# Rows of 320 columns for the feed-forward's split input, and a ten-column tile of ones

## The chip, the cores and the metric

The kernel runs on one core of one Trainium2 chip. The metric is the time of one execution on the device, in microseconds (us). Three executions of the kernel before took 365.12, 365.38 and 365.51 us; the median is 365.38 us.

## The reference

One transformer block on 256 tokens of width 1024, in float32. What matters here is its last part:

```
x = x + gate1 * (merged @ w_out)
h = rmsnorm(x, g_ffn) * (1 + scale2) + shift2
x = x + gate2 * (square(relu(h @ w_ff1)) @ w_ff2)
return rmsnorm(x, g_final)
```

`w_ff1` is 1024 x 4096 and `w_ff2` 4096 x 1024. Ahead of this stand the modulation (six vectors of 1024 out of `c @ w_ada`), the input projection, attention, a spatial gating unit and the two gates `ga` and `gb`, which weigh the outputs of the two branches into `merged`.

## The kernel before

Activations lie transposed: 128 features on the partitions, `KT` = 8 blocks of features, 256 tokens along a row. Each float32 product is made of three products in the format `float32r`: a weight tile `raw` is split into a high part `whi` (a rounded copy, by ACT) and a low part `wlo` (the rest, by DVE), an activation in the same way, and `mm3` issues high x high, low activation x high weight, high activation x low weight into one PSUM bank. The activation is the moving operand, the weights are loaded into the array for each matmul, 128 columns at a time.

The feed-forward's input is `zh` (high) and `zl` (low), one row of each for each block `ko` of features. A row holds 256 tokens and two columns more, `ZW` = 258: column 256 carries the shift of the modulation, so that its product with the weights comes out of the same matmul, and column 257 is zero. (The norm's factor of each token is applied behind the product, in `relu2`.) `zh` and `zl` use the room of `ga_sb` and `gb_sb`, the two gates, by the same tags `b3` and `b4`, and those in turn the room of the tiles `xn` and `xt` of the start.

`ff1(n)` makes 256 of the 4096 hidden features: for each `ko` in order and each half `i` one `mm3`, so six matmuls on row `ko`, 48 in a call, into two banks. `relu2` and `relu2_low` turn the result into `fh` and `fl`, 512 columns of which a matmul reads 256. `ff2(n)` adds their product with 256 rows of `w_ff2` into four banks, again 48 matmuls a call. There are 16 calls of each; past the start they alternate, `ff2(n)` then `ff1(n + 3)`. Instructions of each engine stand in the order in which the text issues them where `InOrder` is pinned, and PE's follows the calls above. `prepare` loads and splits weight tiles two slots ahead, all loads on SP's queue.

The tile `ones` is read in two places: `ones[:, 0:1]` is the moving operand that sums squares over features (`sums`), and `ones[:, 0:2]` is an operand of a first GpSimd operation at the start (L140). Attention and the projections (`wide`, with rows of `hh`, `hl`, `oh`, `yh`, `mh` and others, 256 columns each) run ahead of the feed-forward.

Tiles get their room in the order of the pools: first `const`, in which `ones` lies, then `act` with `b3` and `b4`, then the pools of work tiles and of weights. Each tile begins at a multiple of 32 bytes. What follows a tile moves when its size changes.

Of the kernel before, what the change touches and what calls it, by code (L numbers as in the profile page):

```python
# [9 lines left out]
F32 = mybir.dt.float32  # L10
F32R = mybir.dt.float32r
# [5 lines left out]
P = 128  # L17
S = 256
D = 1024
KT = D // P  # L20
# [27 lines left out]
def block_kernel(ctx, tc, x, xT, cols, wsguT, bsgu, w_a1, w_1, w_a, w_m, w_f, out):  # L48
    nc = tc.nc
    PE, DVE, ACT = (InOrder(tc, e) for e in (nc.tensor, nc.vector, nc.scalar))  # L50
    const = ctx.enter_context(tc.tile_pool(name="const", bufs=1))
    act = ctx.enter_context(tc.tile_pool(name="act", bufs=1))
# [7 lines left out]
    def bank():  # L60
        return ps.tile([P, 512], F32, name="bank", tag="bank")
# [8 lines left out]
    def mm3(out, wh, wl, ah, al, first, last, **kw):  # L70
        PE.matmul(out=out, lhsT=wh, rhs=ah, start=first, stop=False, **kw)
        PE.matmul(out=out, lhsT=wh, rhs=al, start=False, stop=False, **kw)
        PE.matmul(out=out, lhsT=wl, rhs=ah, start=False, stop=last, **kw)
# [24 lines left out]
        for _ in range(n):  # L98
            PE.matmul(out=idle_ps, lhsT=idle[:, 0:P], rhs=idle, start=True, stop=True)

    ones = const.tile([P, P], F32, name="ones")
    DVE.memset(ones, 1.0)
    nhalf = const.tile([P, 2], F32, name="nhalf")
    DVE.memset(nhalf, -0.5)
# [42 lines left out]
    for kt in range(KT):  # L147
        w = slice(P * (kt % 4), P * (kt % 4) + P)
# [128 lines left out]
    for kt in range(KT):  # L277
# [7 lines left out]
        wh = his.tile([P, 2048], F32R, name="whi", tag="whi")  # L285
        wl = los.tile([P, 2048], F32R, name="wlo", tag="wlo")
# [85 lines left out]


    u_sb = act.tile([P, NP, S], F32, name="u_sb", tag="u1")
    ga_sb = act.tile([P, KT, S + 2], F32, name="ga_sb", tag="b3")
    gb_sb = act.tile([P, KT, S + 2], F32, name="gb_sb", tag="b4")
    oh = act.tile([P, NP, S], F32R, name="oh", tag="o1")
    ol = act.tile([P, NP, S], F32R, name="ol", tag="o2")
    yh = act.tile([P, NP, S], F32R, name="yh", tag="q1")
# [2 lines left out]
    def wide(n, ah, al, nk, base=0):  # L382

        wh, wl = parts[n]
        o = bank()
        for ko in range(nk):
            for i in range(2):
                w = slice(base + 256 * ko + P * i, base + 256 * ko + P * i + P)
                mm3(o[:, S * i:S * i + S], wh[:, w], wl[:, w], ah[:, ko], al[:, ko],
                    ko == 0 and i == 0, ko == nk - 1, skip_group_check=i == 1)  # L390
        return o
# [89 lines left out]
    for n in range(10):  # L481
# [26 lines left out]
        o = wide(n, hh, hl, KT)  # L508
# [27 lines left out]
    for j in range(4):  # L536
# [5 lines left out]
        for k, (ah, al, g) in enumerate(((oh, ol, ga_sb), (yh, yl, gb_sb))):  # L542
            o = wide(n, ah, al, 4, 1024 * k)
# [10 lines left out]


    ZW = S + 2
    zh = act.tile([P, KT, ZW], F32R, name="zh", tag="b3")
    zl = act.tile([P, KT, ZW], F32R, name="zl", tag="b4")
    zero = const.tile([P, KT], F32, name="zero")
    nc.gpsimd.memset(zero, 0.0)  # L560
    sq2 = wk.tile([P, S], F32, name="sq2", tag="sqa", bufs=1)
    for j in range(4):
# [5 lines left out]
        o = wide(n, mh, ml, KT)  # L568
# [6 lines left out]
        for ft in fts:  # L575
            i = ft % 2
# [20 lines left out]
    def ff1(n, half=None):  # L597
        wh, wl = parts[n]
        o = [bank(), bank()]
        for ko in range(KT):  # L600
            for i in range(2):
                w = slice(256 * ko + P * i, 256 * ko + P * i + P)
                mm3(o[i][:, 0:ZW], wh[:, w], wl[:, w], zh[:, ko], zl[:, ko], ko == 0, ko == KT - 1)
            if ko == 3 and half:
                half()
        return o
# [41 lines left out]

    prepare(slot + 2)
    f[0] = ff1(slot)  # L650
    sums(ss2, sq2, True, True)
    rs2 = rstd(ss2, D)
    slot += 1
    prepare(slot + 2)
    f[1] = ff1(slot, spread2)
    a[0] = relu2(f.pop(0))
    slot += 1
    prepare(slot + 2)
    a[1] = relu2(f.pop(1))
    a[0] = relu2_low(*a[0])  # L660
    f[2] = ff1(slot)
    slot += 1
    for n in range(NU - 2):
# [113 lines left out]
```

## Time and profile before

| | |
|---|---|
| median of 3 runs | 365.38 us (365.12 to 365.51) |
| profiled execution | 365.32 us, of which its span from first to last instruction is 363.1 us |
| busy share | PE 97%, weight loads 93%, DVE 71%, ACT 60%, GpSimd 3% |
| chain that ended last | PE 80%, DVE 6%, ACT 5%, DMA 3% |
| granted TensorE clock | 0.996 on average |
| DMA | 90.39 MB, 249 GB/s on average |

A busy share is taken over the whole span, in which stages with different limits follow one another. The chain is followed back from the last instruction to what released it, so a long piece of one engine in it is a stretch in which nothing else was waited for. Matmuls overlap in the records (one begins before the one before it has left the array), and their ends are modelled: the pace of PE is read from the distance between starts. L44 is the line of the helper through which the three pinned engines issue, so groups are told apart by the names of their tiles and not by lines.

### The profile page before, as it was taken

Reading aid. Unit: us, or ns where it says so; the run is one execution under the profiler, and the core shown is the slowest. Engines: PE = TensorE matmul, PEld = TensorE weight load, DVE = VectorE, ACT = ScalarE, POOL = GpSimd, SP = SyncE. Lnnn points to the kernel's source line nnn. Section 1 sums busy time; section 2 is a strip of 40 time slices with the busy share of each in tenths; the row PEclk is TensorE's granted clock in tenths of the full one; section 3 lists DMA queues with packets and bytes.
Section 4 is the critical chain, followed back from the end, with each engine's and each line's share of the span. In section 5 each row is a group of like instructions: output and inputs, shape, how many; then the busy total and the mean of one; then the engine's idle time right before and its main releaser. Section 6 shows DMA issues by size and latency. Waiting matters only on the chain.

```text
span 363.1 us, 6942 instructions
## 1 busy us (share of the span) xinstructions
PE 352.5 (97%) x2898; PEld 339.3 (93%) x2898; DVE 259.5 (71%) x397; ACT 216.5 (60%) x308; POOL 9.1 (3%) x16
## 2 busy tenths in 40 slices
PE   6999999999999999999999999999999999999993
PEld 4788888999999999999999999999999999999993
DVE  4889889498799989899858575675755645646443
ACT  4866749899973554546566454565544655446242
POOL 3000000003000000000000000000000000000001
PEclk9999999999999999999999999999999999999998
DMA  7999999789899995568735576755757564500003
GB/s 238 411 414 414 407 326 393 291 305 368 320 350 383 345 361 222 226 237 311 264 135 214 186 280 231 248 216 212 268 217 270 195 231 141 210 2 0 2 0 116
DMA packets 16270, 90.39 MB, mean 249 GB/s; under 512 B 1904, under 2 KB 2416, under 8 KB 7152
## 3 DMA queue, kind: packets, MB, share of 16 engines
q1 hardware_dynamic: 16240, 89.97, 66.6%
q8 instruction: 22, 0.36, 0.4%
q14 instruction: 8, 0.07, 0.0%
HBM read 88.91 MB, written 1.05 MB: 248 GB/s over the span
## 4 chain that ended last, share of the span: by engine, by line
PE 80%; DVE 6%; ACT 5%; DMA 3%; issue 3%; SPq 1%; DVEq 0%; POOLq 0%; POOL 0%
PE bank L44 80%; DVE junk L44 3%; DMA raw<-in_w 2%; ACT whi L44 2%; DVE wlo L44 2%; DMA raw<-in_w_m 1%; ACT hh L44 1%; ACT hf L44 1%; ACT bcol L44 1%; SPq L67 0%; DVE yg L44 0%; DVE x_sb L44 0%; SPq L82 0%; DVE ys L44 0%; POOLq L773 0%
## 5 line engine op out<-in xcount | busy, mean ns | idle before, releaser
L44 ACT CAST whi<-raw 128x2048 fp32r<-128x2048 f32 (+2 forms) x74 | 112.9, 1539 | 76.3 <-PE bank L44 71.8
L44 DVE TENSOR_TENSOR wlo<-raw,whi 128x2048 fp32r<-128x2048 f32 (+2 forms) x74 | 134.4, 1827 | 14.3 <-ACT whi L44 13.9
L44 PE MATMUL bank<-zh,whi 128*128 128x258 f32 x256 | 72.6, 284 | 0.0
L44 PE MATMUL bank<-zl,whi 128*128 128x258 f32 x256 | 72.5, 283 | 0.0
L44 PE MATMUL bank<-zh,wlo 128*128 128x258 f32 x256 | 72.1, 282 | 0.0
L44 PE MATMUL bank<-fh,whi 128*128 128x256 f32 x256 | 70.7, 276 | 0.0
L44 PE MATMUL bank<-fh,wlo 128*128 128x256 f32 x256 | 70.7, 276 | 0.0
L44 PE MATMUL bank<-fl,whi 128*128 128x256 f32 x256 | 70.7, 276 | 0.0
L44 DVE SCALAR_TENSOR_TENSOR junk<-raw,csb 128x1024 bf16<-128x1024 f32 x48 | 57.4, 1218 | 0.4 <-DMA raw<-in_w_a 0.4
L44 PE MATMUL bank<-hh,whi 128*128 128x256 f32 x224 | 55.3, 286 | 1.0 <-ACT hh L44 0.4
L44 PE MATMUL bank<-hl,whi 128*128 128x256 f32 x224 | 53.9, 280 | 0.5 <-DVE hl L44 0.5
L44 PE MATMUL bank<-hh,wlo 128*128 128x256 f32 x224 | 53.6, 279 | 0.0
L44 PEld LDWEIGHTS bank<-zh,wlo 128*128 128x128 f32 x256 | 48.5, 190 | 0.0
L44 PEld LDWEIGHTS bank<-zh,whi 128*128 128x128 f32 x256 | 48.4, 189 | 0.0
L44 PEld LDWEIGHTS bank<-zl,whi 128*128 128x128 f32 x256 | 48.4, 189 | 0.0
L44 PEld LDWEIGHTS bank<-fl,whi 128*128 128x128 f32 x256 | 48.1, 188 | 0.0
L44 PEld LDWEIGHTS bank<-fh,whi 128*128 128x128 f32 x256 | 48.1, 188 | 0.0
L44 PEld LDWEIGHTS bank<-fh,wlo 128*128 128x128 f32 x256 | 48.1, 188 | 0.0
L44 PEld LDWEIGHTS bank<-hh,whi 128*128 128x128 f32 x224 | 38.2, 188 | 5.2 <-ACT hh L44 4.2
L44 PEld LDWEIGHTS bank<-hl,whi 128*128 128x128 f32 x224 | 38.4, 189 | 1.0 <-DVE hl L44 0.9
L44 PEld LDWEIGHTS bank<-hh,wlo 128*128 128x128 f32 x224 | 38.2, 188 | 0.1
L44 DVE TENSOR_TENSOR fl<-r,fh 128x512 fp32r<-128x512 f32 x16 | 11.1, 692 | 27.4 <-PE bank L44 26.1
(143 smaller groups left out, 476.8 us busy)
## 6 DMA issues: line engine op xcount, KB each, us to landing
raw<-in_w_f SPq DMA_DIRECT2D x32, 1024.0 KB, 4.8
raw<-in_w_a SPq DMA_DIRECT2D x22, 1024.0 KB, 6.9
raw<-in_w_m SPq DMA_DIRECT2D x16, 1024.0 KB, 5.7
raw<-in_w SPq DMA_DIRECT2D x12, 512.0 KB, 9.4
raw<-in_w_a SPq DMA_DIRECT2D x4, 512.0 KB, 6.7
raw<-in_w SPq DMA_DIRECT2D x8, 256.0 KB, 6.7
xt<-in_x SPq DMA_DIRECT2D x2, 512.0 KB, 3.9
raw<-in_w_m SPq DMA_DIRECT2D x4, 256.0 KB, 5.9
```

The source lines that it names most:

```text
L44: return lambda *a, **k: pin(op(*a, **k))
```

## The change

The tiles `ga_sb`, `gb_sb`, `zh` and `zl` become 320 columns wide instead of 258, and the matmuls of `ff1` read columns 0 to 257 of a row by a slice. A row is then 1280 bytes instead of 1032. `ones` has ten columns instead of 128. Each of the tags `b3` and `b4` grows by 8 x 62 x 4 = 1984 bytes in a partition; `ones` with its rounding shrinks by 448. No instruction is added, taken away or moved on any engine; one memset is shorter.

```
-    ones = const.tile([P, P], F32, name="ones")
+    ones = const.tile([P, 10], F32, name="ones")
     DVE.memset(ones, 1.0)
...
-    ga_sb = act.tile([P, KT, S + 2], F32, name="ga_sb", tag="b3")
-    gb_sb = act.tile([P, KT, S + 2], F32, name="gb_sb", tag="b4")
+    ga_sb = act.tile([P, KT, S + 64], F32, name="ga_sb", tag="b3")
+    gb_sb = act.tile([P, KT, S + 64], F32, name="gb_sb", tag="b4")
...
     ZW = S + 2
-    zh = act.tile([P, KT, ZW], F32R, name="zh", tag="b3")
-    zl = act.tile([P, KT, ZW], F32R, name="zl", tag="b4")
+
+    zh = act.tile([P, KT, S + 64], F32R, name="zh", tag="b3")
+    zl = act.tile([P, KT, S + 64], F32R, name="zl", tag="b4")
...
-                mm3(o[i][:, 0:ZW], wh[:, w], wl[:, w], zh[:, ko], zl[:, ko], ko == 0, ko == KT - 1)
+                mm3(o[i][:, 0:ZW], wh[:, w], wl[:, w], zh[:, ko, 0:ZW], zl[:, ko, 0:ZW], ko == 0, ko == KT - 1)
```

## Rows read from the trace of the kernel before

**Rows 1.** The page: busy us (share of the span) and instructions of each engine.

```profile
span 363.1 us, 6942 instructions
PE 352.5 (97%) x2898; PEld 339.3 (93%) x2898; DVE 259.5 (71%) x397; ACT 216.5 (60%) x308; POOL 9.1 (3%) x16
```

**Rows 2.** The chain in order of time: start us, us, what.

```profile
155.95 195.52 PE bank L44 x1676
```

**Rows 3.** Who waited for whom: us in total, times, longest us.

```profile
DVE bw L44 <- PE bank L44: 35.3, 15, 2.6
```

**Rows 4.** Groups by shape, ff1 and ff2: count, busy us, mean ns, idle before.

```profile
L44 PE MATMUL bank<-zh,whi 128*128 128x258 f32 x256 | 72.6, 284 | 0.0
...
L44 PE MATMUL bank<-fh,whi 128*128 128x256 f32 x256 | 70.7, 276 | 0.0
```

**Rows 5.** Timeline of PE, one ff1 call, each row's first matmul: start, us.

```profile
219.78 0.29 PE L44 MATMUL bank<-zh,whi 128*128 128x258 f32 x1
...
220.51 0.28 PE L44 MATMUL bank<-zh,whi 128*128 128x258 f32 x1
...
221.22 0.28 PE L44 MATMUL bank<-zh,whi 128*128 128x258 f32 x1
...
221.93 0.28 PE L44 MATMUL bank<-zh,whi 128*128 128x258 f32 x1
...
222.66 0.28 PE L44 MATMUL bank<-zh,whi 128*128 128x258 f32 x1
...
223.37 0.28 PE L44 MATMUL bank<-zh,whi 128*128 128x258 f32 x1
...
224.10 0.28 PE L44 MATMUL bank<-zh,whi 128*128 128x258 f32 x1
...
224.81 0.29 PE L44 MATMUL bank<-zh,whi 128*128 128x258 f32 x1
...
225.54 0.28 PE L44 MATMUL bank<-fh,whi 128*128 128x256 f32 x1
...
231.00 0.29 PE L44 MATMUL bank<-zh,whi 128*128 128x258 f32 x1
```

**Rows 6.** Timeline of PE, two calls of wide on hh and hl.

```profile
74.34 0.28 PE L44 MATMUL bank<-hl,whi 128*128 128x256 f32 x1
...
79.76 0.28 PE L44 MATMUL bank<-hh,wlo 128*128 128x256 f32 x1
...
98.71 0.28 PE L44 MATMUL bank<-hh,whi 128*128 128x256 f32 x1
...
103.13 0.28 PE L44 MATMUL bank<-hh,whi 128*128 128x256 f32 x1
```

**Rows 7.** Timeline of PE, third ff1 call, first matmul of rows 0 and 1.

```profile
186.14 0.28 PE L44 MATMUL bank<-zh,whi 128*128 128x258 f32 x1
...
186.88 0.28 PE L44 MATMUL bank<-zh,whi 128*128 128x258 f32 x1
```

**Rows 8.** Groups by shape, DVE and ACT on the widened tiles and on others.

```profile
L44 ACT ACTIVATE zh<-x_sb,acol 128x256 fp32r<-128x256 f32 x8 | 3.6, 498 | 0.0
...
L44 DVE TENSOR_TENSOR yg<-yg 128x512 f32<-128x512 f32 x4 | 2.7, 685 | 0.0
...
L44 DVE SCALAR_TENSOR_TENSOR yg<-ga_sb,bank 128x512 f32<-128x512 f32 x4 | 2.7, 681 | 0.0
L44 ACT ACTIVATE yg<-x_sb,cols_sb 128x256 f32<-128x256 f32 x6 | 2.7, 495 | 0.0
```

**Rows 9.** The tile zh: durations min/median/max ns, first and last start.

```profile
L44 PE MATMUL bank<-zh,whi x256: 278/282/366, 173.7 to 337.3; 128*128 128x258 f32 x128
...
L44 DVE TENSOR_TENSOR zl<-bcol,zh x1: 163/163/163, 173.3 to 173.3; 128x8 fp32r<-128x8 f32 x1
```

**Rows 10.** Timeline of the start: start us, us, idle before.

```profile
1.23 0.17 DVE L44 MEMSET ones<- 128x128 f32 x1
...
1.35 0.06 DVE L44 MEMSET nhalf<- 128x2 f32 x1
...
2.80 0.17 DVE L44 SCALAR_TENSOR_TENSOR cs<-cs,cols_sb 128x8 f32<-128x8 f32 x1 [1.12 <-ACT cs L44]
```

## The prediction

> **What bounds the kernel now.** I read the page first, then the chain in order of time, then the groups of instructions with shapes kept apart, and last the timeline of TensorE alone. The page says which engine is full: PE is busy for 352.5 of 363.1 us, and DVE, the next, for 259.5 [rows 1]. A busy share does not yet say that PE sets the end; the chain does. Its last long piece is PE's own, 195.52 us from 155.95 on, with no other engine between [rows 2]. The whole feed-forward lies in that piece, so every nanosecond that one of its matmuls takes or loses there is a nanosecond of the run. The other engines wait for PE and not the reverse: DVE's reading of the feed-forward's first product waits 35.3 us in all for PE [rows 3].
>
> The change touches one of the two kinds of matmul in that piece. The first product, ff1, streams the rows of zh and zl, 258 columns each; the second, ff2, streams fh and fl, 256 columns. There are 3 x 256 = 768 of each, and the groups list 284 ns against 276 ns [rows 4]. These are modelled ends; the distance from one start to the next is the cost. One ff1 call runs from 219.78 to 225.54, 48 matmuls in 5.76 us or 120.0 ns each, and the ff2 call behind it to 231.00, 5.46 us or 113.8 ns each [rows 5]. For two more columns of 256 that is much: columns alone would make 120.0 out of 113.3 x 258 / 256 = 114.2 (the 113.3 is the steady pace of 256 columns: 39 matmuls from 98.71 to 103.13 [rows 6]). So 5.8 ns for each of 768 matmuls, 4.4 us, are in ff1 for a reason other than their columns. The question of this case is whether that reason is where the rows begin.
>
> **The change, part by part.**
>
> The rows of zh and zl. A row was 258 x 4 = 1032 bytes, 16 x 64 + 8; in the addresses that the built program gives, both tiles begin at a multiple of 64 bytes, before and after. So row ko began 8 x ko bytes past a 64-byte line, and row 0 began on one. With 1280 = 20 x 64 bytes all eight do. The matmuls, their number, their 258 columns and their order stay. That makes a test inside the trace of before: row 0 is already what all rows will be. An ff1 call takes six matmuls for each row in order, and the rows' first starts are 219.78, 220.51, 221.22, 221.93, 222.66, 223.37, 224.10, 224.81, then ff2 at 225.54 [rows 5]. Six matmuls take 0.73, 0.71, 0.71, 0.73, 0.71, 0.73, 0.71, 0.73 us. The aligned row 0 is among the dearest, 0.73 us or 121.7 ns each, and row 4, half a line off, is among the cheapest. The six matmuls of row 0 stand right behind ff2 matmuls at the steady pace, so no misaligned row went before them. In the third call, where row 0 follows another ff1 call, it takes 186.14 to 186.88, 0.74 us [rows 7]. If the start cost 5.8 ns, row 0 would take 0.685 us; it takes 0.73. Line counts say the same: a row of 1032 bytes that begins 0, 8, ... 56 bytes past a 64-byte line touches 17 lines in each case, and 17 after the change.
>
> What the pace of 120 ns then comes from, no row shows. A 258th column that opens a further 64-byte line would fit (16 lines at 113.3, 17 at 120.4), and it stays. So I take 0 ns for each matmul, the reading of row 0 and of the mean together. The bounds: below, all 5.8 ns go, 768 x 5.8 = 4.4 us; above, every row goes at row 0's pace, 121.7 instead of 120.0, 768 x 1.7 = +1.3 us (rounding of the starts lets row 0 lie anywhere from 120 to 123 ns).
>
> [...]
>
> [...] The trace is less simple: equal matmuls of 256 columns with the same tiles run at 113.3 ns in one stretch and, from 74.34 to 79.76, 46 of them, at 117.8 ns in another [rows 6]. PE has a second, slower pace, which it keeps once it is in it; that makes a rival too.
>
> Rows of ga_sb and gb_sb get the same 320 columns. ACT writes two rows of 256 at once and DVE reads two. DVE's read of rows that lie apart takes 681 ns, and an operation of the same size on contiguous rows 685 [rows 8]: the distance between rows costs nothing, and 1280 is no other kind of distance than 1032. Likewise ACT's write of a zh row, 498 ns at all eight offsets on average, against 495 for an aligned tile of the same shape [rows 8]: 0, and the bound is these 3 ns, on an engine that waits for PE.
>
> The two extra columns of zh and zl are written with a step of a row, now 1280 bytes. The last is 163 ns on DVE and starts at 173.3 [rows 9]; the first ff1 matmul starts at 173.7 [rows 9], and the one behind it is the first to read zl, 0.12 us later. The write would have to take over 0.5 us to delay PE. 0.
>
> The tile of ones. Its memset of 128 columns takes 0.17 us, and one of two columns 0.06 [rows 10]. At most 0.11 us earlier on DVE in the first 1.4 us; the next thing PE needs from DVE, cs, starts only at 2.80, after ACT, which waits for a load. So 0, bound -0.1 us. Only columns 0 and 1 are ever read.
>
> Addresses. Everything behind these tiles moves up by 3520 bytes, a multiple of 64. No instruction is added, taken away or moved on any engine, and no DMA.
>
> Sum: 365.32 us, the profiled execution's own time (its span of 363.1 and 2.2 around it), plus 0. The median of three runs is 365.38; forecast 365.4, its own range 365.0 to 365.8.
>
> **The rivals.**
>
> (a) The start does cost the excess, and row 0 does not show it because PE needs more than six matmuls to come back to its pace. For it: 256 columns whose rows all begin on a line go at 113.3. Against it: row 0 at 0.73 us, in two calls with different work before. If all rows reach 114.2 ns the run is 4.4 us shorter: 361.0. If they only reach PE's slower pace, 117.8 x 258 / 256 = 118.7, it is 1.3 x 768 = 1.0 us: 364.4.
>
> (b) The other side: with eight rows at one distance from a line, each call repeats row 0's pattern instead of mixing eight, and the pace settles above the mean. At row 0's own pace +1.3 us, 366.7. If it settles in the slower pace, 117.8 - 113.3 = 4.5 ns on each of 768 is +3.5 us: 368.9. For it: that pace exists, with aligned rows [rows 6]. Against it: behind the ff1 calls ff2 is at 113.8 at once. It decides the sign from 0.95 ns a matmul on (0.73 us, 0.2%).
>
> (c) The change does not do what it says: the excess is in 258 columns, not in where they begin. This is my forecast.
>
> **How the numbers follow.** Unchanged 0.50. (a) 0.26: 0.18 for all, 0.08 for the part. (b) 0.24: 0.10 at row 0's pace, 0.14 at the slower one. A change of 0.2% is 0.73 us, about what a measurement can tell here. So faster 0.26, same 0.50, slower 0.24. The range goes from 360.7 (the full gain with the memset's 0.1 and its rounding) to 366.8; it leaves out the slower pace, 0.14.
>
> **What would show it.** If right, an ff1 call of the changed kernel still takes 5.76 us for its 48 matmuls, an ff2 call 5.46, with rows' steps more alike than 0.71 and 0.73. If (a), a call takes about 5.48 us and its matmuls' listed duration falls from 284 towards 277 ns. If (b), a call takes 5.84 us or more, or ff2 shows 117 ns. I am wrong if row 0 is no sample of a row that follows aligned rows: seven steady rows may let PE reach a pace that six matmuls do not.

## The result, and the profile after

The changed kernel took 369.31 us (median of 6 executions, 368.38 to 370.42), the kernel before 365.25 us beside it (6, 364.52 to 365.55). The ratio is 1.011, 95% interval 1.0091 to 1.0129: 4 us slower. The profiled execution took 368.38 us.

The page of the changed kernel shows the same instructions on the same engines as [rows 1], and PE busy 3.2 us longer:

```profile
span 366.3 us, 6942 instructions
PE 355.7 (97%) x2898; PEld 342.9 (94%) x2898; DVE 259.3 (71%) x397; ACT 216.4 (59%) x308; POOL 9.4 (3%) x16
```

The chain of the changed kernel in order of time (start, us, what) has the same last long piece as [rows 2], and it has grown from 195.52 us to this:

```profile
155.25 199.29 PE bank L44 x1676
```

So the loss lies in the feed-forward and on PE. Its groups by shape (count, busy us, mean ns, idle before) say in which of the two products:

```profile
L44 PE MATMUL bank<-zh,whi 128*128 128x258 f32 x256 | 72.8, 284 | 0.0
...
L44 PE MATMUL bank<-fh,whi 128*128 128x256 f32 x256 | 72.0, 281 | 0.0
```

Against [rows 4], ff1 has stayed at 284 ns and ff2 has gone from 276 to 281, though the change touches no operand of ff2. The timeline of PE in the changed kernel, one ff1 call and the ff2 call behind it (start, us), answers to [rows 5]:

```profile
219.90 0.28 PE L44 MATMUL bank<-zh,whi 128*128 128x258 f32 x1
...
220.62 0.28 PE L44 MATMUL bank<-zh,whi 128*128 128x258 f32 x1
...
225.70 0.28 PE L44 MATMUL bank<-fh,whi 128*128 128x256 f32 x1
...
231.36 0.28 PE L44 MATMUL bank<-zh,whi 128*128 128x258 f32 x1
```

ff1 takes 5.80 us for 48 matmuls, 120.8 ns each, where it took 5.76; ff2 takes 5.66 us, 117.9 ns each, where it took 5.46. That is (120.8 - 120.0) x 768 = 0.6 us in ff1 and (117.9 - 113.8) x 768 = 3.1 us in ff2. It is not the clock: the same two stretches in windows (length, PE busy, granted clock, DMA share, GB/s) both have a granted clock of 1.00:

```profile
219.90:225.70 5.80, 5.80 (x50) 1.00 0.43 144
225.70:231.36 5.66, 5.66 (x51) 1.00 0.61 229
```

So have the two of [rows 5] in the kernel before:

```profile
219.78:225.54 5.76, 5.76 (x50) 1.00 0.45 168
225.54:230.99 5.45, 5.45 (x50) 1.00 0.63 215
```

117.9 ns is the slower pace that [rows 6] showed for equal matmuls in another stage, 117.8 ns there. The question for the experiments was what puts ff2 into it.

### The profile page after: what moved, and what is told of

It reads as the page before. It is cut to its first block, busy times and chain, and to the rows that moved or that the text cites. A ratio compares the mean times of both kernels' runs of the same rounds, so it can differ in the third digit from the quotient of the medians.

```text
span 366.3 us, 6942 instructions
## 1 busy us (share of the span) xinstructions
PE 355.7 (97%) x2898; PEld 342.9 (94%) x2898; DVE 259.3 (71%) x397; ACT 216.4 (59%) x308; POOL 9.4 (3%) x16
## 4 chain that ended last, share of the span: by engine, by line
PE 79%; DVE 7%; ACT 6%; DMA 4%; issue 3%; POOLq 0%; POOL 0%; DVEq 0%; SPq 0%
PE bank L44 79%; DVE junk L44 3%; ACT whi L44 2%; DVE wlo L44 2%; DMA raw<-in_w_a 2%; DMA raw<-in_w_m 1%; ACT hh L44 1%; ACT hf L44 1%; ACT pr L44 1%; ACT bcol L44 0%; DMA cols_sb<-in_cols 0%; DVE yg L44 0%; DVE x_sb L44 0%; POOLq L774 0%; DVE ys L44 0%
## 5 line engine op out<-in xcount | busy, mean ns | idle before, releaser
L44 PE MATMUL bank<-fh,whi 128*128 128x256 f32 x256 | 72.0, 281 | 0.0
L44 PE MATMUL bank<-fh,wlo 128*128 128x256 f32 x256 | 71.9, 281 | 0.0
L44 PE MATMUL bank<-fl,whi 128*128 128x256 f32 x256 | 71.9, 281 | 0.0
L44 PEld LDWEIGHTS bank<-fl,whi 128*128 128x128 f32 x256 | 49.2, 192 | 0.0
```

What stands on the lines that cost most here:

```text
L44: return lambda *a, **k: pin(op(*a, **k))
```

## The experiments

Start distances below are from the timelines of PE. A listed mean of 276 or 277 ns for ff2 goes with a distance of 113.3 to 113.8 ns, and 281 with 117.7 to 117.9. The granted clock is 1.00 in windows from 60 to 349 us of the kernel before and of the changed kernel, and from 173.2 to 345.3 us of the last run; over the whole of each other profiled execution its mean is 0.993 to 0.997. Each time stands beside executions of the kernel before on the same chip.

**The ones tile alone.**

```
-    ones = const.tile([P, P], F32, name="ones")
+    ones = const.tile([P, 10], F32, name="ones")
```

> The ones tile alone is cut to ten columns; rows of zh and zl stay 258 wide, so they begin 0, 8, ... 56 bytes past a 64-byte line as before, while every later tile moves by 448 bytes. Theory A (hand-over: PE has two paces for 256-column matmuls, 113.3 and 117.8 ns, keeps the one it is in, and what the rows of ff1 leave behind decides which one ff2 takes up): ff1 120.0 ns, ff2 113.5 ns a matmul, 365.3 us. Theory B (addresses: it is the move of the weight tiles and of fh and fl by an odd multiple of 64 bytes that slows ff2, not the rows of zh): ff2 117.8 ns, about 368.7 us.

364.96 us against 365.48, ratio 0.9983 (0.9965 to 1.0001): no change that can be measured. Its groups by shape:

```profile
L44 PE MATMUL bank<-zh,whi 128*128 128x258 f32 x256 | 72.6, 284 | 0.0
...
L44 PE MATMUL bank<-fh,whi 128*128 128x256 f32 x256 | 70.7, 276 | 0.0
```

ff2 keeps 276 ns. The addresses of the weights and of fh and fl, moved by 448 bytes (an odd multiple of 64, as in the change), are not the cause: theory B falls, and the memset's 0.1 us was worth nothing that can be measured, as forecast.

**Rows of 274 and of 272 columns.** Wide rows that begin off a line, and wide rows that begin on one, each with the old ones tile.

```
-    zh = act.tile([P, KT, S + 64], F32R, name="zh", tag="b3")
+    zh = act.tile([P, KT, S + 18], F32R, name="zh", tag="b3")
```

(zl, ga_sb and gb_sb likewise; S + 16 in the second kernel.)

> Rows of 274 columns, 1096 bytes = 17 x 64 + 8: wide rows as in the change, but begun 0, 8, ... 56 bytes past a line; ones keeps 128 columns and later tiles move by a multiple of 128 bytes. Theory A: as before the change, ff1 120.0 ns, ff2 113.5 ns, 365.3 us. Theory B: also 365.3 us, since nothing moved by half of 128 bytes. If width or room alone were the cause, ff2 117.8 ns and about 369 us.

> Rows of 272 columns, 1088 bytes = 17 x 64: every row begins on a 64-byte line as in the change; ones keeps 128 columns and later tiles move by a multiple of 128 bytes. Theory A: as after the change, ff1 120.8 ns, ff2 117.8 ns, about 369.3 us. Theory B: ff2 113.5 ns, 365.3 us.

274 columns: 368.75 us, ratio 1.0095 (1.0067 to 1.0123). 272 columns: 368.90 us, ratio 1.0099 (1.0071 to 1.0126). The groups of the kernel with 274:

```profile
L44 PE MATMUL bank<-zh,whi 128*128 128x258 f32 x256 | 72.5, 283 | 0.0
...
L44 PE MATMUL bank<-fh,whi 128*128 128x256 f32 x256 | 71.9, 281 | 0.0
```

Both have ff2 at 281 ns. Theory A had said fast behind rows off the line and slow behind rows on it. That half falls with the first kernel: its rows begin at the same eight distances from a line as before the change, and ff2 is slow all the same. What came in both is the outcome written down for "width or room alone": with 258 columns read, rows of 272, 274 or 320 columns were each enough to make ff2 slow (281 ns), whether they begin on a line or off it. How the rows of zh and zl reach a stage that does not read them is what is left of A, the hand-over.

**256 columns in ff1, on and off the line.**

```
-                mm3(o[i][:, 0:ZW], wh[:, w], wl[:, w], zh[:, ko, 0:ZW], zl[:, ko, 0:ZW], ko == 0, ko == KT - 1)
+                mm3(o[i][:, 0:S], wh[:, w], wl[:, w], zh[:, ko, 0:S], zl[:, ko, 0:S], ko == 0, ko == KT - 1)
```

> The changed kernel with ff1's matmuls cut to 256 columns (left out: the product of the shift with the weights; relu2 reads column 255 in its place). If the excess of ff1 lies in the two columns past 256 and not in the rows' start: ff1 at 113.3 ns (or at the slower pace of 117.8), so at least 768 x 3 = 2.3 us less than the changed kernel and at best 768 x (120.8 - 113.3) + 768 x (117.8 - 113.3) = 9.2 us less, 360.1 us. Theory A: with 256 columns everywhere PE keeps one pace through ff1 and ff2, both 113.3 or both 117.8. If the excess were in something else of ff1: 120 ns stays, 369 us.

> The kernel before with ff1's matmuls cut to 256 columns (left out: the product of the shift with the weights; relu2 reads column 255 in its place), its rows still 258 wide, so that they begin 0, 8, ... 56 bytes past a 64-byte line and rows 1 to 7 touch 17 lines, row 0 16. If a start off the line costs anything, or each line touched does: rows 1 to 7 at about 120 ns, row 0 at 113.3, ff1 like before, 365 us. If the excess of ff1 is in its two columns past 256: ff1 at 113.3 ns on all rows (or at the slower pace of 117.8), about 360.2 us.

On the line (the changed kernel's rows): 360.25 us, ratio 0.9864 (0.9834 to 0.9895). Off the line (the rows of before): 364.15 us, ratio 0.9968 (0.9956 to 0.998). The timeline of PE on the line, an ff1 call and an ff2 call:

```profile
218.57 0.28 PE L44 MATMUL bank<-zh,whi 128*128 128x256 f32 x1
...
224.01 0.28 PE L44 MATMUL bank<-fh,whi 128*128 128x256 f32 x1
...
229.45 0.28 PE L44 MATMUL bank<-zh,whi 128*128 128x256 f32 x1
```

Both take 5.44 us, 113.3 ns a matmul, and so do all later calls: this is the best case that was written down, 360.1 us. It is not so from the start. The first ff1 call of the same kernel, on the same rows, runs at the slower pace, 48 matmuls in 5.65 us or 117.7 ns each:

```profile
173.83 0.28 PE L44 MATMUL bank<-zh,whi 128*128 128x256 f32 x1
...
179.48 0.50 PE L44 MATMUL bank<-ones,sq 128*128 128x1 f32 x4
```

And off the line, with row 0's six matmuls first:

```profile
219.20 0.28 PE L44 MATMUL bank<-zh,whi 128*128 128x256 f32 x1
...
219.91 0.29 PE L44 MATMUL bank<-zh,whi 128*128 128x256 f32 x1
...
224.91 0.28 PE L44 MATMUL bank<-fh,whi 128*128 128x256 f32 x1
```

Here ff1 takes 5.71 us, 119.0 ns a matmul, and row 0, which does begin on a line, takes 0.71 us like the others, 118.3 ns. So how the rows lie does count: 5.6 ns a matmul between two kernels whose ff1 matmuls have the same length (1.2 ns where the first of them is at its slower pace). And row 0 does not show it, though the 48 ff2 matmuls ahead of it are at 113.3 ns and it begins on a line. Neither of the two outcomes written down for the second kernel came: not row 0 fast and the others slow, and not all fast. Since even row 0 is slow, a cost that each matmul pays for its own start is not shown. The two kernels differ in more than where rows begin: zl lies 8 x 1032 = 129 x 64 bytes from zh in one and 8 x 1280 = 160 x 64 in the other, and no run parts the two. Nor does any run show that 64 bytes is the unit that counts.

**One cut matmul between ff1 and ff2.** The first matmul of ff2 in two pieces, in the changed kernel and in the kernel before.

```
+                if n > 0 and len(fts) == KT and ft == 0 and i == 0:
+                    for c in (slice(0, P), slice(P, S)):
+                        PE.matmul(out=o[:, c], lhsT=wh[:, w], rhs=fh[:, i, c], start=False, stop=False)
...
```

> The changed kernel with the first matmul of each ff2 call from the second to the fourteenth cut into two of 128 columns: same tiles, same rows, one matmul more (about 0.1 us) between ff1 and the rest of ff2. Theory H (PE's pace is a state that it keeps, and what it meets between ff1 and ff2 decides which one ff2 gets): some or all of these calls leave 117.8 ns for 113.3; if all do, 13 x (48 x 4.4 - 110) ns = 1.3 us less than the changed kernel, 368.0 us. Theory L (where rows and tiles lie sets the pace of ff2 itself): 117.8 ns stays everywhere, 13 x 0.11 = 1.4 us more than the changed kernel, 370.7 us.

> The same cut of the first ff2 matmul in the kernel before, whose ff2 calls are at 113.5 ns already. Theory H: nothing to win, 1.4 us more from the added matmuls, 366.7 us, and up to 2.7 us on top in calls that now fall into 117.8 ns. Theory L: 113.5 ns stays, 366.7 us.

In the changed kernel: 367.25 us, ratio to the kernel before 1.0056 (1.0034 to 1.0078), about 2 us less than the changed kernel's 369.31, with a matmul more in 13 calls. In the kernel before: 369.70 us, ratio 1.0116 (1.0096 to 1.0136). PE's timeline in the changed kernel with the cut, from the first fh,wlo matmul behind the cut one to the call's last (45 matmuls):

```profile
214.64 0.34 PE L44 MATMUL bank<-fh,whi 128*128 128x128 f32 x2
214.82 0.34 PE L44 MATMUL bank<-fl,whi 128*128 128x256 f32 x1
214.99 0.28 PE L44 MATMUL bank<-fh,wlo 128*128 128x256 f32 x1
...
220.09 0.28 PE L44 MATMUL bank<-fh,wlo 128*128 128x256 f32 x1
```

5.10 us for 45 matmuls is 113.3 ns: the fast pace. The same stretch in the kernel before with the cut:

```profile
215.00 0.28 PE L44 MATMUL bank<-fh,wlo 128*128 128x256 f32 x1
...
220.31 0.28 PE L44 MATMUL bank<-fh,wlo 128*128 128x256 f32 x1
```

5.31 us for 45 is 118.0 ns. The first ff2 call, which is not cut, is a control in each of the two executions. In the changed kernel with the cut it lasts from the first of these lines to the second, 5.65 us for 48 matmuls, and stays slow:

```profile
191.82 0.28 PE L44 MATMUL bank<-fh,whi 128*128 128x256 f32 x1
...
197.47 0.28 PE L44 MATMUL bank<-zh,whi 128*128 128x258 f32 x1
```

In the kernel before with the cut it stays fast (191.92 to 197.38, 5.46 us). The same cut turns slow calls fast and fast calls slow, with every tile of ff2 where it was. That is what theory H said: the pace of ff2 came from what stood ahead of it and was kept to the end of the call (45 matmuls at 113.3 or 118.0 ns), and is not a property of ff2's tiles. The last two ff2 calls, not cut themselves but right behind a cut one, keep its pace too, for 96 matmuls more in either kernel.

**The low part of the shift in zh's spare column,** so that zl needs 256 columns.

```
-            DVE.tensor_tensor(out=zl[:, :, S], in0=bcol[:, 1], in1=zh[:, :, S].bitcast(F32), op=ALU.subtract)
+            DVE.tensor_tensor(out=zh[:, :, S + 1], in0=bcol[:, 1], in1=zh[:, :, S].bitcast(F32), op=ALU.subtract)
...
+                PE.matmul(out=o[i][:, 0:S], lhsT=wh[:, w], rhs=zl[:, ko, 0:S], start=False, stop=False)
```

> The kernel before with the low part of the shift in column 257 of zh, where a zero stood, so that zl's matmuls need 256 columns only; relu2 adds columns 256 and 257. It computes the reference. If the two columns cost 6.7 ns in each matmul that has them: 256 of 768 matmuls are rid of them, 1.7 us less, 363.6 us, with ff2 at 113.5 ns. Theory H: the mixture of lengths may hand ff2 the slower pace instead, +3.4 us, 367.0 us.

365.44 us, ratio 1.0006 (0.9985 to 1.0027). A miss for the first reading: the shorter third of ff1 brings nothing that can be measured, and ff2 is not slow either. zl's matmuls are listed at 282 ns against 283 for zh's, ff2 at 277. That the mixture of lengths keeps all three uneven is not shown: the rows still begin off the line, where even 256 columns throughout took 119.0 ns against 120.0. A third of that is 256 x 1.0 ns = 0.3 us, too little to see; the 6.7 ns of the expectation is the gain on the line.

**Longer matmuls on the line: 272, 264 and 260 columns.**

```
-    ZW = S + 2
+    ZW = S + 16
```

(S + 8 and S + 4 in the other two; the columns past the shift's are zeros.) 256 columns from a line, 16 whole lines of 64 bytes, had kept one pace, 113.3 ns from the third call on. The question here is whether 17 whole lines do so too, and what a half or a quarter of a line does.

> Rows of 272 columns, each begun on a 64-byte line, and ff1's matmuls read all 272 (17 whole lines): columns 257 to 271 are zeros, written once. It computes the reference; ones keeps 128 columns. [...] Rival N (any length over 256 costs 120 and irregular starts): ff1 irregular at 120 to 124 ns, ff2 at either pace.

> The same with matmuls of 264 columns (16 lines and a half). [...] If half lines (32 bytes) count as whole: regular, 114 to 117 ns, ff2 at 113.3 or 117.8 ns. 362 to 369 us.

> The same with matmuls of 260 columns (16 lines and a quarter). [...] If quarter lines (16 bytes) count as whole: regular, 113.3 to 115 ns, ff2 at 113.3 or 117.8 ns: 361 us at best. Rival N: 120 ns or a little more.

| columns | ff1, listed ns of zh,whi | ff2, listed ns of fh,whi | time, us | ratio |
|---|---|---|---|---|
| 272 | 286 | 276 | 368.98 | 1.0094 (1.0077 to 1.0111) |
| 264 | 286 | 281 | 369.14 | 1.0104 (1.0083 to 1.0125) |
| 260 | 283 | 276 | 365.47 | 0.9996 (0.9975 to 1.0017) |

The timeline of the kernel with 272:

```profile
220.68 0.28 PE L44 MATMUL bank<-zh,whi 128*128 128x272 f32 x1
220.80 0.29 PE L44 MATMUL bank<-zl,whi 128*128 128x272 f32 x1
...
226.68 0.28 PE L44 MATMUL bank<-fh,whi 128*128 128x256 f32 x1
...
232.12 0.28 PE L44 MATMUL bank<-zh,whi 128*128 128x272 f32 x1
```

6.00 us for 48 is 125.0 ns, above the 113.3 x 272 / 256 = 120.4 that the pace of 256 columns would make of 272, an estimate: that a matmul ends on a line does not keep the pace. Rival N had an uneven stream right (listed means of 286, 289 and 288 ns for its three kinds of matmul, where ff2 lists 276 for each) and the size for 272 too low (120 to 124 ns); 264 at 121.4 and 260 at 120.3 fit it, and lie above what half lines (114 to 117) and quarter lines (113.3 to 115) would have given if they counted as whole. And ff2 is fast behind 272 and 260 and slow behind 264: which pace is handed over follows no rule that these runs show. "Slow where the matmul reads less than its row" fits the six other layouts in which every ff1 matmul is longer than 256 columns and fails for 260 columns in rows of 272.

**A version that the runs point to.** ff1 with rows of 256 on the line and nothing else in the row: the shift has to go into the row. The first five calls stay as they are: the token factor comes out only during the second, and eight rows have to be written behind it.

```
+            DVE.scalar_tensor_tensor(out=t, in0=x_sb[:, ft], scalar=acol[:, 1, ft:ft + 1], in1=rb2,
+                                     op0=ALU.mult, op1=ALU.mult)
+            ACT.activation(out=z2h[:, ft], in_=t, func=AF.Identity, bias=bcol[:, 1, ft:ft + 1])
+            DVE.scalar_tensor_tensor(out=z2l[:, ft], in0=t, scalar=bcol[:, 1, ft:ft + 1],
+                                     in1=z2h[:, ft].bitcast(F32), op0=ALU.add, op1=ALU.subtract)
...
+                    mm3(o[i][:, 0:S], wh[:, w], wl[:, w], z2h[:, ko], z2l[:, ko], ko == 0, ko == KT - 1)
```

> A version that the runs point to; it computes the reference. From the sixth ff1 call on, ff1 reads other tiles, z2h and z2l, which hold the whole normed input (token factor and shift folded in, eight rows written by DVE and ACT while PE is at the third ff1 and the first ff2 call), 256 columns a row, each begun on a 64-byte line; relu2 of these calls is a maximum with 0. If 256 whole columns from a line let PE keep its pace: these 11 ff1 calls run at 113.3 ns with ff2 at 113.3 too, 11 x 48 x 6.7 ns = 3.5 us less than before, 361.8 us. If the pace handed over is the slower one: both at 117.8 ns from there on, 11 x 48 x (4.4 - 2.2) ns = 1.2 us more than before, 366.5 us. If the eight rows are late or crowd DVE, PE waits in the sixth ff1 call and some of the gain goes.

361.27 us against 365.07, ratio 0.99 (0.9884 to 0.9917): about 1% faster than the kernel before. Its timeline of PE, one of the eleven calls:

```profile
219.24 0.28 PE L44 MATMUL bank<-z2h,whi 128*128 128x256 f32 x1
...
224.68 0.28 PE L44 MATMUL bank<-fh,whi 128*128 128x256 f32 x1
...
230.12 0.28 PE L44 MATMUL bank<-z2h,whi 128*128 128x256 f32 x1
```

5.44 us for both, 113.3 ns. By the tile z2l (min/median/max ns, first and last start), its last row is written at 201.0, 18 us ahead of the first read:

```profile
L44 DVE SCALAR_TENSOR_TENSOR z2l<-zt,bcol,z2h x8: 476/480/485, 185.1 to 201.0; 128x256 fp32r<-128x256 f32 x8
```

So the added work is hidden, and the gain is 3.8 us where 11 x 48 x 6.7 ns = 3.5 were expected. In this kernel the weights, fh and fl lie where they lie in the kernel before, so their places are not what keeps 256 columns off the line at 119.0 ns.

## Why the prediction was wrong

**The step that failed** is "The change touches one of the two kinds of matmul in that piece". From there on ff2 stood in the sum as a constant, 113.8 ns, on the sole ground that its operands and instructions did not change. It measured 117.9: 3.1 of the 3.7 us that the two calls show, 16 times over. The slower pace was seen ahead [rows 6], and the second half of rival (b) had its price, 4.5 ns on 768 matmuls or 368.9 us, and its sign, "or ff2 shows 117 ns". That is what came, though (b) tells it of ff1's rows: only ff2 stands near the 113.3 ns that its price starts from. But it was given 0.14 and left out of the range, and its evidence against, "behind the ff1 calls ff2 is at 113.8 at once", took for a property of ff2 what was the outcome of one hand-over. The cut matmul in the kernel before shows how little stood behind it.

The condition that (b) gave, eight rows at one distance from a line, is not the cause: rows of 274 columns begin at eight distances, and ff2 is slow behind them too. What put ff2 into the slower pace is shown as far as the wider rows; why wider rows hand it over stays open.

**Rows of zh and zl at 0 ns.** The size was nearly right: 120.0 became 120.8 ns, +0.6 us, inside the bound of +1.3. The reason was not. Row 0 was read as a sample of an aligned row, and the run with 256 columns off the line shows that it is none: there row 0 is as slow as its neighbours (118.3 ns, 119.0 over the call), while with all rows on the line every row is at 113.3 from the third call on. The closing sentence of the forecast named this way of being wrong. That the change brought nothing in ff1 all the same fits two conditions that have to hold at once. Off the line with 256 columns is 119.0 ns, on the line with 258 is 120.8, on the line with 256 is 113.3 or, in the first call, 117.7. The change met one of the two. So the 0 came out nearly right in part by luck. The first half of rival (b), a settling above the mean, came in part: in the changed kernel all eight rows take 0.72 or 0.73 us, 120.8 ns a matmul against 120.0.

**Line counts.** "A 258th column that opens a further 64-byte line would fit": it did not hold. 272 columns touch 17 lines as 258 do, and take 125.0 ns; and off the line with 256 columns row 0, with 16 lines, takes 118.3.

**Where the rows lie.** Equal matmuls of 256 columns took 113.3 or 119.0 ns by how their rows lie. That a place has no effect on a matmul is shown by no run; the 0 for the rows was the author's estimate from row 0 and the mean. What a run does show is that one move of later tiles, by 448 bytes, was worth nothing that can be measured (364.96 us against 365.48).

In one layout, rows of 272 columns, 12 columns more cost 125.0 - 120.3 = 4.7 ns, 0.39 ns a column. The 113.3 / 256 = 0.44 ns a column by which the prediction scaled agrees roughly with that slope; the whole, 120.4 ns for 272 columns by that scale, does not agree with the 125.0 measured.

**The chain.** "The whole feed-forward lies in that piece" goes a little too far: the piece of [rows 2] ends at 155.95 + 195.52 = 351.47, and the last ff2 matmul starts at 353.9. These last 2.4 us run beside the chain; the sum does not change by it.

**The small terms.** ones, the gates' rows and the columns with a step of a row were put at 0. The run with ones alone agrees for the first; the other two were not measured apart.

**The profiled execution** is only 3.1 us above that of before, the medians 4.1. Its feed-forward starts 0.7 us earlier (first ff1 matmul at 173.06 against 173.74), and the last piece of the chain grew by 3.8 us. Of the 0.7, 0.2 is the same choice of pace, fallen otherwise in another stage: the changed kernel's wide call at 81.30 was, in that execution, at the fast pace where before it was at the slow one (46 matmuls in 5.22 us and 5.42 us). The rest was not followed.

**What stays open.** What in PE keeps a pace, and why 256 columns from a line were steady and 260 or 272 were not. Whether it is where rows begin or the distance from zh to zl that makes 256 columns uneven. Which hand-over gives which pace: the layouts with uneven ff1 calls gave fast or slow without a rule that fits all. None was changed in a single row only, which might tell.

## What to carry to other kernels

When PE sets the end, read the distance between matmul starts for every kind of matmul, also those that a change leaves alone: a stage can lose because of what ran just before it (here ff2, 5.46 us a call before and 5.66 after, on operands that did not change). Stretches of equal matmuls at two distances in one profile are a warning that a layout change can make PE choose again, here for 4% of that stage (117.8 against 113.3 ns). Here it paid to give the operands of a long chain of matmuls one length and one alignment that had been seen steady (256 columns on a line, 113.3 ns), and not to widen a row by two columns to save an extra pass: 361.27 us against 365.07.

## What the runs showed of the hardware that was not expected

- Equal float32r matmuls of 256 columns ran at two steady paces, 113.3 and 117.8 ns, both at a granted clock of 1.00, and kept one for a whole run of them (39 and 46 matmuls in two calls of wide, 48 in an ff2 call).
- A single matmul cut in two between the stages switched ff2 from one to the other, in either direction (117.9 to 113.3 ns in the changed kernel, 113.8 to 118.0 in the kernel before).
- With rows of 258 columns, seven of eight of which begin off a 64-byte line, or with matmuls of 258 to 272 columns, an ff1 call took means of 119.0 to 125.0 ns a matmul. The steps are uneven: 0.11 to 0.13 us in one call of 258 columns, 0.11 and 0.12 in the ff2 call behind it.
- 256 columns in rows that all begin on a 64-byte line were even throughout, at either pace (117.7 ns in the first call, 113.3 from the third on).
- A third of ff1's matmuls made shorter (256 among 258), with rows off the line, saved nothing that can be measured: 365.44 us against 365.40.
